# Row sums of squares for the input RMSNorm: from transposed tiles, vector additions and matmuls with ones, to a token-major load with ScalarE's row sums

## The chip, the core and the metric

The kernel runs on one core of a Trainium2 chip. The metric is the device time of one execution in microseconds (us). A core has five engines with a queue each: TensorE (PE in the profile, with its weight loads as PEld), VectorE (DVE), ScalarE (ACT), GpSimd (POOL) and SyncE (SP, which here only issues DMAs). Each engine takes its instructions in the order in which the program holds them; an instruction that waits for a semaphore holds up everything behind it in its queue.

## The reference, cut to what matters

One step of a one-layer encoder with two mixing branches (retention and sliding-window attention), cross attention and SwiGLU, for 1024 prompt tokens and 64 sample tokens, each of 1024 features, in fp32. The change touches only the first norm:

```
def rms_norm(x, g=None):
    y = xf * lax.rsqrt(jnp.mean(xf * xf, axis=-1, keepdims=True) + EPS)
    if g is not None:
        y = y * g
xn = rms_norm(x, g_attn); rq, rk, rv, rg, sq, sk, sv, ga, gb = split(xn @ w_in)
```

So for each of the 1088 tokens one number is wanted, 1 / sqrt(mean of squares + 1e-6). It is a factor per token, and a projection is linear, so the kernel projects x times the gains and multiplies by this factor later.

## The kernel before, in words

The activations lie transposed: features on the 128 partitions, tokens along the row, 8 tiles of 128 x 1088 (T = 1088 tokens; HALF = 544, HC = 272). fp32 products are made of three passes: `split` writes a high part by a ScalarE copy (L123) and a low part by a VectorE subtraction (L124), and TensorE multiplies high by high, high by low and low by high (L222, L223, L225). Each pair of weight blocks of 1024 x 128 goes through seven block products of Strassen's kind (`strassen`; the products are called P1, P2, P6, P5, P7, P3, P4 in the order in which they run). One product is 24 matmuls into a pair of PSUM banks (tile pq), of which three pairs exist. Its operands are the halves of x (tiles B.., T..) and a weight operand `wq` that VectorE's sums (L190, L192, L195, L196) and the split have made from two raw tiles (`raw`, two buffers, filled by SP's DMAs). The results are taken by VectorE (u, L269, and stage, L609); for queries and keys the rotary products follow on VectorE (L640 to L646).

`project_phase` runs: values of head 0, keys of head 0 (w_k), **token_squares**, queries of head 0 (w_q), **token_roots** and `retention_setup`, the retention of head 0 and **spread_roots**, then for each further head its keys, queries, values and SWA queries and its retention, then the gates. What is produced goes by DRAM (d_qkv) to the retention, which loads it in blocks of 256 tokens (ks, qs, vf), transposes keys and values on TensorE (pk) and multiplies them by token factors (`tok`, made of `rtok`) on their way out of PSUM.

The order in which the engines get these instructions isn't that of the code. `build` makes the context with `schedule_with_timeline_sim=True`: a scheduler places every instruction in its engine's queue by its own estimate of times, `rsqrt` under `high_priority`, some pieces tied by `issue_after`. A tile of a pool with `bufs=1` and a tag has one buffer, and a load into it waits until the last reader of the former tile of that tag is done.

The norm's part before the change: `token_squares` loads x a second time from xT in 16 tiles of 128 x 544 (into the buffers of the retention's kt, vb, ss, st), ScalarE squares them (L487), and VectorE adds 14 of them into `rstd` (L489; the first of each half is written there directly), so that rstd holds 128 partial sums for each token. `token_roots` adds over the partitions and turns tokens onto partitions at once, with nine matmuls of rstd against a column of ones (L498, tile pt), and takes the roots (`rsqrt`: L309 VectorE, L310 ScalarE's Sqrt with its table load, L311 to L314 VectorE) into `rtok` (token on the partition, nine columns). `spread_roots` (L508, L510) later spreads rtok back over the partitions into rstd.

Of the kernel before, what the change touches and what calls it, by code (L numbers as in the profile page):

```python
# [11 lines left out]
F32 = mybir.dt.float32  # L12
F32R = mybir.dt.float32r
AF = mybir.ActivationFunctionType
ALU = mybir.AluOpType
# [4 lines left out]
P = 128  # L20
D = 1024
KT = D // P
SEQ = 1024
SMP = 64
# [16 lines left out]
HALF = T // 2  # L41
# [68 lines left out]
class Kernel:  # L110
# [366 lines left out]

    def token_squares(self):

        nc, tags = self.nc, ("kt", "vb", "ss", "st")  # L480
        for t in range(2):
            hs = slice(t * HALF, (t + 1) * HALF)
            for k in range(KT):
                x = self.ra.tile([P, HALF], F32, tag=tags[k % 4], bufs=1, name="xsq")
                self.load(x, self.io["xT"][k, :, hs])
                acc = self.rstd[:, hs]
                nc.scalar.activation(x if k else acc, x, AF.Square)  # L487
                if k:
                    nc.vector.tensor_tensor(out=acc, in0=acc, in1=x, op=ALU.add)  # L489

    def token_roots(self):

        nc = self.nc
        ps = self.norm_psum("pt")
        pv = ps[:, :18].rearrange("p (t two) -> p t two", two=2)
        for i in range(9):
            w = P if i < 8 else SMP
            nc.tensor.matmul(pv[:w, i, :], self.rstd[:, i * P:i * P + w], self.ones[:, :2], start=True, stop=True)  # L498
        self.rsqrt(self.rtok[:, :8], pv[:, :8, 0], D)
        self.rsqrt(self.rtok[:SMP, 8:], pv[:SMP, 8:, 0], D)  # L500

    def spread_roots(self):

# [1342 lines left out]
```

## Time and profile before

| what | value |
|---|---|
| median of three runs | 2179.87 us (2178.16 to 2180.32) |
| the profiled execution, its own time | 2174.66 us |
| its span, first to last instruction | 2172.7 us |
| TensorE busy, of the span | 2140.9 us (99%) |
| TensorE weight loads busy | 2088.6 us (96%) |
| VectorE, ScalarE, GpSimd busy | 72%, 40%, 26% |
| mean granted TensorE clock | 0.995 |

The profiled execution is 5.21 us below the median of the runs, and its span ends 1.96 us below its own time. A busy share is an average: 99% of TensorE says that the program is a stream of matmuls nearly without holes. A matmul is shown with some 0.29 us, but the next one starts 0.125 us after it, since they are pipelined; so time lost on TensorE is read from the starts, not from the durations. The names of rows are those of the program without buffer numbers (pq<-T,wq is a product into pq of operands T and wq).

### The profile page before, as it was taken

The page shows a single profiled execution, that of the slowest core. Times are in us where ns is not written, and L with a number is a line of the kernel's source. Part 1 is how long each engine was busy: PE and PEld are TensorE (multiplying, and loading weights), DVE is VectorE, ACT ScalarE, POOL GpSimd, SP SyncE. Part 2 cuts the span into 40 slices and gives each one's busy share as a digit, 9 for nine tenths or more (in the row PEclk, how much of TensorE's full clock was granted, in tenths as well). Part 3 has the DMA queues.
Part 4 walks back from the last instruction along what each step waited for, and adds up shares of the span by engine and source line. Part 5 has one row for each costly group of instructions (what it writes and reads, how often), then busy time and mean ns, then how long its engine had stood idle before and what let it go on. Part 6 is the DMA issues. An engine that isn't in the chain of part 4 may idle for free.

```text
span 2172.7 us, 41775 instructions
## 1 busy us (share of the span) xinstructions
PE 2140.9 (99%) x16389; PEld 2088.6 (96%) x16389; DVE 1555.6 (72%) x2884; ACT 876.0 (40%) x1898; POOL 559.1 (26%) x438
## 2 busy tenths in 40 slices
PE   9999999999999999999999999999999999999997
PEld 9999999999999997889999999999999999999997
DVE  8996879776677667656545565768777776777588
ACT  7344344344344356653233343333222322344243
POOL 0000311132243223430000000015555555523531
PEclk9999999999999999999999999999999999999999
DMA  6433444445345477327443111422343333394333
GB/s 208 162 130 106 141 133 120 141 131 154 112 145 174 163 220 222 122 77 228 130 155 103 40 57 51 153 81 91 126 133 105 105 98 119 100 328 138 125 109 119
DMA packets 181446, 290.83 MB, mean 134 GB/s; under 512 B 40291, under 2 KB 109315, under 8 KB 181251
## 3 DMA queue, kind: packets, MB, share of 16 engines
q1 hardware_dynamic: 176130, 278.18, 40.5%
q10 hardware_dynamic: 4608, 8.36, 1.0%
q8 instruction: 129, 2.11, 0.4%
q0 software_dynamic: 512, 1.64, 0.2%
q14 instruction: 67, 0.54, 0.1%
HBM read 196.95 MB, written 91.16 MB: 133 GB/s over the span
## 4 chain that ended last, share of the span: by engine, by line
PE 72%; DVE 4%; DMA 2%; issue 2%; ACT 1%; POOL 1%; SPq 0%; POOLq 0%; DVEq 0%; ACTq 0%
PE pq L225 14%; PE pq L222 14%; PE pq L223 14%; PE pd L156 8%; PE pd L158 8%; PE pd L157 8%; PE pss L984 1%; PE pout L1047 1%; DVE wq L124 1%; PE pp L1023 1%; DMA ld<-d_swa 0%; DVE y L1577 0%; PE css L157 0%; PE css L156 0%; PE css L158 0%
## 5 line engine op out<-in xcount | busy, mean ns | idle before, releaser
L124 DVE TENSOR_TENSOR wq<-raw,wq 128x512 fp32r<-128x512 f32 (+1 forms) x499 | 440.1, 887 | 120.5 <-ACT wq L123 116.9
L123 ACT CAST wq<-raw 128x512 fp32r<-128x512 f32 (+1 forms) x499 | 301.7, 613 | 523.9 <-PE pq L225 206.0
L222 PE MATMUL pq<-T,wq 128*128 128x272 f32 x1832 | 490.9, 288 | 2.3 <-ACT wq L123 2.0
L223 PE MATMUL pq<-T,wq 128*128 128x272 f32 x1832 | 491.5, 288 | 0.0
L223 PE MATMUL pq<-B,wq 128*128 128x272 f32 x1592 | 427.5, 289 | 1.9 <-DVE B L124 1.7
L222 PE MATMUL pq<-B,wq 128*128 128x272 f32 x1592 | 426.1, 288 | 0.5 <-ACT B L123 0.4
L225 PE MATMUL pq<-T,wq 128*128 128x272 f32 x1832 | 382.3, 289 | 1.6 <-DVE wq L124 1.6
L222 PEld LDWEIGHTS pq<-T,wq 128*128 128x128 f32 x1832 | 344.2, 188 | 3.6 <-ACT wq L123 2.1
L223 PEld LDWEIGHTS pq<-T,wq 128*128 128x128 f32 x1832 | 344.1, 188 | 0.8 <-issue 0.8
L225 PE MATMUL pq<-B,wq 128*128 128x272 f32 x1592 | 332.9, 289 | 0.0
L223 PEld LDWEIGHTS pq<-B,wq 128*128 128x128 f32 x1592 | 299.7, 188 | 2.9 <-DVE B L124 2.5
L222 PEld LDWEIGHTS pq<-B,wq 128*128 128x128 f32 x1592 | 299.5, 188 | 1.4 <-ACT B L123 0.9
L225 PEld LDWEIGHTS pq<-T,wq 128*128 128x128 f32 x1832 | 289.3, 189 | 3.3 <-DVE wq L124 2.0
L200 POOL TENSOR_TENSOR raw<-raw 128x512 f32<-128x512 f32 (+1 forms) x44 | 63.4, 1442 | 829.1 <-DVE rs_r L311 483.5
L225 PEld LDWEIGHTS pq<-B,wq 128*128 128x128 f32 x1592 | 252.3, 190 | 0.8 <-issue 0.8
L269 DVE TENSOR_TENSOR u<-pq,u 128x544 f32<-128x544 f32 x177 | 127.2, 719 | 90.0 <-PE pq L225 90.0
L615 POOL TENSOR_TENSOR stage<-stage,rstd 128x544 f32<-128x544 f32 x20 | 32.2, 1616 | 341.3 <-ACT rstd L510 216.6
L609 DVE TENSOR_TENSOR stage<-pq,u 128x544 f32<-128x544 f32 x112 | 80.4, 718 | 35.8 <-PE pq L225 27.4
L156 PE MATMUL pd<-xc,wq 128*128 128x256 f32 (+1 forms) x256 | 74.5, 291 | 0.0
L158 PE MATMUL pd<-xc,wq 128*128 128x256 f32 (+1 forms) x256 | 74.1, 289 | 0.0
L1495 POOL TENSOR_TENSOR stage<-stage,rstd_f 128x544 f32<-128x544 f32 x40 | 63.9, 1608 | 39.1 <-ACT stage L1494 39.1
L157 PE MATMUL pd<-xc,wq 128*128 128x256 f32 (+1 forms) x256 | 73.7, 288 | 0.0
(387 smaller groups left out, 4568.2 us busy)
## 6 DMA issues: line engine op xcount, KB each, us to landing
hl<-d_op SPq DMA_DIRECT2D x85, 272.0 KB, 5.2
d_qkv<-stage SPq DMA_DIRECT2D x44, 272.0 KB, 2.1
d_op<-stage SPq DMA_DIRECT2D x44, 272.0 KB, 2.2
d_op<-ht SPq DMA_DIRECT2D x44, 272.0 KB, 3.4
raw<-w_gate SPq DMA_DIRECT2D x22, 512.0 KB, 3.5
raw<-w_up SPq DMA_DIRECT2D x22, 512.0 KB, 4.0
raw<-w_down SPq DMA_DIRECT2D x16, 512.0 KB, 5.1
d_gate<-stage ACTq DMA_DIRECT2D x28, 272.0 KB, 3.0
```

What stands on the lines that cost most here:

```text
L123: self.last_cast = self.nc.scalar.copy(hi, src).ins
L124: return self.nc.vector.tensor_tensor(out=lo, in0=src, in1=hi.bitcast(F32), op=ALU.subtract).ins
L156: mm(ps, wh, xh, start=start, stop=False)
L157: mm(ps, wh, xl, start=False, stop=False)
L158: self.last_mm = mm(ps, wl, xh, start=False, stop=stop).ins
L200: tt(out=a11, in0=a11, in1=a21, op=sub)
L222: mm(ps[:, c, :HC], w[:, 0, ks], x[:, 0, cs], start=start, stop=False)
L223: mm(ps[:, c, :HC], w[:, 0, ks], x[:, 1, cs], start=False, stop=False)
L225: self.last_mm = mm(ps[:, c, :HC], w[:, 1, ks], x[:, 0, c * HC:(c + 1) * HC], start=False, stop=stop).ins
L269: add = lambda out, a, b: nc.vector.tensor_tensor(out=out, in0=a, in1=b, op=ALU.add)
L609: nc.vector.tensor_tensor(out=o, in0=ps, in1=sb, op=ALU.add)
L1495: nc.gpsimd.tensor_tensor(out=g, in0=g, in1=r[t], op=ALU.mult)
```

## The change

x is given to the program a second time with tokens on the rows (`x`, 1088 x 1024, made on the host beside xT). `token_squares` loads it in nine tiles of 128 tokens x 1024 features (the last of 64 tokens), five buffers in turn (kt, vb, st, ks, qs in place of kt, vb, ss, st), and one ScalarE instruction for each squares it and writes the row sums into a column of rtok. `token_roots` takes the roots in place. The 14 additions on VectorE and the nine matmuls with ones are gone, and so is the PSUM tile pt.

```diff
     def token_squares(self):
-        nc, tags = self.nc, ("kt", "vb", "ss", "st")
-        for t in range(2):
-            hs = slice(t * HALF, (t + 1) * HALF)
-            for k in range(KT):
-                x = self.ra.tile([P, HALF], F32, tag=tags[k % 4], bufs=1, name="xsq")
-                self.load(x, self.io["xT"][k, :, hs])
-                acc = self.rstd[:, hs]
-                nc.scalar.activation(x if k else acc, x, AF.Square)
-                if k:
-                    nc.vector.tensor_tensor(out=acc, in0=acc, in1=x, op=ALU.add)
-
-    def token_roots(self):
-        nc = self.nc
-        ps = self.norm_psum("pt")
-        pv = ps[:, :18].rearrange("p (t two) -> p t two", two=2)
+        nc, tags = self.nc, ("kt", "vb", "st", "ks", "qs")
         for i in range(9):
             w = P if i < 8 else SMP
-            nc.tensor.matmul(pv[:w, i, :], self.rstd[:, i * P:i * P + w], self.ones[:, :2], start=True, stop=True)
-        self.rsqrt(self.rtok[:, :8], pv[:, :8, 0], D)
-        self.rsqrt(self.rtok[:SMP, 8:], pv[:SMP, 8:, 0], D)
+            x = self.ra.tile([P, D], F32, tag=tags[i % 5], bufs=1, name="xsq")[:w]
+            self.load(x, self.io["x"][i * P:i * P + w])
+            nc.scalar.activation(x, x, AF.Square, accum_out=self.rtok[:w, i:i + 1])
+
+    def token_roots(self):
+        for r in (self.rtok[:, :8], self.rtok[:SMP, 8:]):
+            self.rsqrt(r, r, D)
...
+    arr["x"] = x
     arr["xT"] = np.ascontiguousarray(x.T).reshape(KT, P, T)
```

The scheduler places the instructions anew from there on. On SP, POOL, DVE and ACT the order differs from token_squares to the end of the third head's retention, and after it only in a swap or two; the matmuls are the same but for the nine. Lines behind token_squares have numbers lower by ten in the changed kernel. Three places matter below.

SP's queue behind the rope table: the loads of x (xsq), the mask and the first values of the retention, and the two raw tiles of the queries' weights (w_q). Before, and then with the change:

```order
L117 DMA rope<-c_rope 128x2x544 x2
L117 DMA xsq<-xT 128x544 x4
L117 DMA dm<-c_dmask 128x448
L117 DMA vf<-d_qkv 128x2x256
L117 DMA xsq<-xT 128x544 x2
L117 DMA raw<-w_q 128x1024 x2
L117 DMA xsq<-xT 128x544 x7
```

```order
L117 DMA rope<-c_rope 128x2x544 x2
L117 DMA xsq<-x 128x1024 x5
L117 DMA dm<-c_dmask 128x448
L117 DMA vf<-d_qkv 128x2x256
L117 DMA xsq<-x 128x1024 x2
L117 DMA raw<-w_q 128x1024 x2
L117 DMA xsq<-x 128x1024
L117 DMA xsq<-x 64x1024
```

Ahead of w_q stand seven loads of 512 KB where six of 272 KB stood, and behind it two where ten stood.

ScalarE's queue from the second group of squares to the roots; raw_825 and raw_790 are the first raw tile of w_q, wq_829 and wq_794 the operand of its first product P1, wq_837 and wq_802 that of P6. Before, and then with the change:

```order
L487 ACTIVATE xsq_770<-xsq_770 128x544
L487 ACTIVATE xsq_774<-xsq_774 128x544
L487 ACTIVATE xsq_778<-xsq_778 128x544
L487 ACTIVATE xsq_782<-xsq_782 128x544
L123 CAST wq_829<-raw_825 128x512
L123 CAST wq_833<-raw_825 128x512
L487 ACTIVATE xsq_786<-xsq_786 128x544
L487 ACTIVATE xsq_790<-xsq_790 128x544
L487 ACTIVATE rstd_68<-xsq_794 128x544
L487 ACTIVATE xsq_809<-xsq_809 128x544
L123 CAST wq_837<-raw_825 128x512
```

```order
L485 ACTIVATE xsq_778,rtok_71<-xsq_778 128x1024
L485 ACTIVATE xsq_781,rtok_71<-xsq_781 128x1024
L123 CAST wq_794<-raw_790 128x512
L123 CAST wq_798<-raw_790 128x512
L485 ACTIVATE xsq_784,rtok_71<-xsq_784 128x1024
L485 ACTIVATE xsq_787,rtok_71<-xsq_787 64x1024
L310 ACT_TABLE_LOAD
L310 ACTIVATE rtok_71<-rs_v_1022 128x8
L123 CAST wq_802<-raw_790 128x512
L123 CAST wq_805<-raw_792 128x512
```

The casts of w_q's P1 and P2 stand behind the seventh square (four more of the same kind stand ahead of the two shown), and the ninth square, the table load and the root have moved ahead of the cast for P6.

VectorE's queue around the same operands; pq_695 and pq_729 are the last two products of w_k. Before, and then with the change:

```order
L489 TENSOR_TENSOR rstd_68<-rstd_68,xsq_778 128x544
L124 TENSOR_TENSOR wq_829<-raw_825,wq_829 128x512
L124 TENSOR_TENSOR wq_833<-raw_825,wq_833 128x512
L641 TENSOR_TENSOR stage1_553<-stage0_552,rope_557 128x544
L190 TENSOR_TENSOR raw_827<-raw_827 128x512
L489 TENSOR_TENSOR rstd_68<-rstd_68,xsq_782 128x544
L609 TENSOR_TENSOR stage0_552<-pq_695,u5_563 128x544
L643 TENSOR_TENSOR stage0_552<-stage0_552,rope_557 128x544
L192 TENSOR_TENSOR raw_825<-raw_827,raw_825 128x512
L489 TENSOR_TENSOR rstd_68<-rstd_68,xsq_786 128x544
L609 TENSOR_TENSOR stage1_553<-pq_729,u3_562 128x544
```

```order
L599 TENSOR_TENSOR stage1_553<-pq_729,u3_562 128x544
L635 TENSOR_TENSOR stage0_552<-stage0_552,stage1_553 128x544
L124 TENSOR_TENSOR wq_794<-raw_790,wq_794 128x512
L124 TENSOR_TENSOR wq_798<-raw_790,wq_798 128x512
L190 TENSOR_TENSOR raw_792<-raw_792 128x512
L631 TENSOR_TENSOR stage1_553<-stage1_553,rope_557 128x544
L309 TENSOR_SCALAR rs_v_1022<-rtok_71 128x8
L192 TENSOR_TENSOR raw_790<-raw_792,raw_790 128x512
L633 TENSOR_TENSOR stage1_553<-stage1_553,rope_557 128x544
L309 TENSOR_SCALAR rs_v_1030<-rtok_71 64x1
L635 TENSOR_TENSOR stage0_552<-stage0_552,stage1_553 128x544
L311 RECIPROCAL rtok_71<-rtok_71 128x8
```

The low part of P1's operand (wq_829, now wq_794) stood ahead of the taking of w_k's last two products; now it stands behind the last of them (pq_729) and one rotary sum. The first steps of the root (L309, L311) have come up between w_q's operands.

## The prediction, made before the changed kernel was run

> **What bounds the kernel now.** I read the page's busy times, then the busy time by stage, then who TensorE waits for, and then the order of time at each place that the change touches.
>
> ```profile
> PE 2140.9 (99%) x16389; PEld 2088.6 (96%) x16389; DVE 1555.6 (72%) x2884; ACT 876.0 (40%) x1898; POOL 559.1 (26%) x438
> 50.00:100.00 50.00, 50.00 (x404) 49.97 (x404) 50.00 (x88) 20.43 (x36) 0.00 (x0) 1.00 0.52 172
> L489 DVE TENSOR_TENSOR rstd<-rstd,xsq 128x544 f32<-128x544 f32 x14 | 10.1, 719 | 0.5 <-ACT xsq L487 0.5
> ...
> 62.18 0.72 DVE L609 TENSOR_TENSOR stage<-pq,u 128x544 f32<-128x544 f32 x1
> 62.82 0.71 DVE L640 TENSOR_TENSOR stage<-stage,rope 128x544 f32<-128x544 f32 x1
> ```
>
> TensorE is the bound of the whole. In the stretch of the changed code, 50 to 100 us, TensorE and VectorE (third busy figure) are both full, ScalarE has 20 of 50 us and GpSimd nothing. VectorE's rows of this shape follow each other after 0.64 us (62.18, 62.82), so the 14 additions hold it for 14 x 0.64 = 9.0 us. A full VectorE costs only where TensorE waits for it, and it does so just behind this stretch:
>
> ```profile
> 111.00 0.41 PE L225 MATMUL pq<-B,wq 128*128 128x272 f32 x2
> 112.14 0.39 PE L222 MATMUL pq<-T,wq 128*128 128x272 f32 x1 [0.72 <-ACT wq L123]
> ...
> 114.52 0.28 PE L223 MATMUL pq<-T,wq 128*128 128x272 f32 x1
> 115.44 0.51 PE L225 MATMUL pq<-T,wq 128*128 128x272 f32 x2 [0.63 <-DVE wq L124]
> ```
>
> The cadence would have put these starts at 111.25 and 114.65 (0.125 us a matmul), so 0.89 and 0.79 us are lost, 1.7 us in all: a queries' operand of the second head is late because VectorE is behind.
>
> **Removed from TensorE: the nine matmuls with ones.**
>
> ```profile
> 67.28 0.95 PE L498 MATMUL pt<-ones,rstd 128*128 128x2 f32 x8
> 68.08 0.50 PE L225 MATMUL pq<-T,wq 128*128 128x272 f32 x2
> 68.42 0.29 PE L222 MATMUL pq<-T,wq 128*128 128x272 f32 x1
> ...
> 89.67 1.16 PE L498 MATMUL pt<-ones,rstd 128*128 128x2 f32 x10
> 90.75 0.52 PE L225 MATMUL pq<-T,wq 128*128 128x272 f32 x2
> 91.11 0.28 PE L222 MATMUL pq<-T,wq 128*128 128x272 f32 x1
> ```
>
> They are 18 passes in two groups. From start to start the groups take 0.80 and 1.08 us, and the pair behind each 0.34 and 0.36 instead of 0.25: 2.1 us of slots. TensorE waits for nothing there, so I take all: **-2.1 us**. It is worth 0 only if VectorE, not TensorE, sets the pace through this stretch; the 9.0 us taken off VectorE in the same stretch speak against that.
>
> **Removed from VectorE: 9.0 us.** It lies beside TensorE's work and counts by what it lets catch up, the 1.7 us above: between -1.7 and 0. In the new order no addition stands ahead of these operands and I count the queue as caught up: **-1.7 us**. The rest of the 9.0 becomes idle time of VectorE.
>
> **Moved on VectorE: w_q's first operand.** TensorE's rows around the border of w_k and w_q, and VectorE's split of P1 and P2 and its last taking of w_k before:
>
> ```profile
> 56.60 1.29 DVE L124 TENSOR_TENSOR wq<-raw,wq 128x512 fp32r<-128x512 f32 x2
> ...
> 60.06 0.41 PE L225 MATMUL pq<-T,wq 128*128 128x272 f32 x2
> 60.31 0.29 PE L222 MATMUL pq<-B,wq 128*128 128x272 f32 x1
> ```
>
> The split was 3.7 us early. Now it stands behind the taking of w_k's last product, which can't start before that product is out: its last pair starts at 60.06 and ends by 60.47, and a signal's time later is 60.6. Then 0.64 (L599), 0.64 (L635) and 0.69 for the split itself give 62.55. TensorE starts w_q at 60.31 with high parts; P1 and P2 are interleaved in fours, so the low part is wanted after eight matmuls, at 61.3. A wait of 62.55 - 61.3 = **+1.25 us**. Behind this split on VectorE stand P2's split and L190, which are wanted later. Its lower end is 0, if the scheduler's pieces slip by each other; the upper end hangs on the loads, next.
>
> **Moved on SP and ScalarE: can w_q be cast in time?**
>
> ```profile
> 47.70 0.66 ACT L487 ACTIVATE rstd<-xsq 128x544 f32<-128x544 f32 x1 [2.05 <-DMA xsq<-xT]
> 55.90 1.14 ACT L123 CAST wq<-raw 128x512 fp32r<-128x512 f32 x2 [1.90 <-DMA raw<-w_q]
> 87.55 1.28 ACT L310 ACT_TABLE_LOAD   x1
> L310 ACT ACTIVATE rtok<-rs_v 128x8 f32<-128x8 f32 x1 | 0.2, 211 | 4.1 <-DVE rs_v L309 4.1
> L870 ACT ACTIVATION_READ_ACCUMULATOR ret_o<-po 128x1 f32 x32 | 6.3, 197 | 0.0
> 41.00:63.00 22.00, 22.00 (x177) 21.98 (x177) 21.42 (x35) 11.17 (x19) 0.00 (x0) 1.00 0.79 268
> 45.00:50.00 5.00, 5.00 (x42) 4.97 (x41) 4.45 (x8) 2.92 (x7) 0.00 (x0) 1.00 1.01 363
> rope<-c_rope SPq DMA_DIRECT2D x2, 544.0 KB, 4.2
> xsq<-xT SPq DMA_DIRECT2D x16, 272.0 KB, 3.5
> d_qkv<-stage SPq DMA_DIRECT2D x11, 272.0 KB, 2.1
> ks<-d_qkv SPq DMA_DIRECT2D x2, 256.0 KB, 3.8
> ```
>
> No row shows a square of 1024 elements. 8 elements take 0.21 us and 544 take 0.66, so 0.84 ns for each, and 1024 take 1.06 us, with 0.2 for the read of the sum 1.26; twice the 544 gives 1.5. Ahead of w_q's first tile SP now sends the rope table (1.11 MB), seven tiles of x (3.67), mask and values (0.49), 5.8 MB with that tile itself. At 363 GB/s, what the fullest five microseconds moved, from 42.5 on (the first issue at 40.5 and 2 us), it lands at 58.5; at 268, the mean of 41 to 63 with idle gaps in it, at 64.1. I take 363 to 350, about 59, because the queue never runs dry: five tiles are sent at once, and the sixth and seventh wait only for the first two squares. Before, the first square began at 47.70 behind 1.39 MB; now 0.25 MB later, 48.3. Then 1.3 for it, three casts of w_k (1.7), and six squares at 1.3 end at 59.1. The casts follow at 59.2 and end by 60.3, when TensorE wants them: +0 us.
>
> P6's operand hangs on a longer chain, since L309 waits for the eighth square ahead of L192, and L311 for ScalarE's root behind the ninth square and the table load: 62 for the eighth tile, 64.6 for two squares, 1.28 + 0.2 to 66.1, then L311, L195, L636 and the split at 0.64 each, 68.4. TensorE wants that low part after 40 more matmuls and eight, at 62.55 + 5 + 1 = 68.5. So +0, without room: each microsecond by which the last loads of x come later than this is one of TensorE.
>
> The keys' store and load again for the first retention block: its last sum on VectorE ends at 67.7, store 2.1, load 3.8 give 73.8 with issue; TensorE reaches the transposes, now inside w_q's products, at 74.0. **+0.2 us**, between 0 and 1.5.
>
> **Everything behind, 120 to 520 us.** The retention of three heads is threaded anew between the products. What TensorE waits for there today:
>
> ```profile
> PE po L156 <- DVE ret_t L884: 1.4, 2, 1.2
> PE po L156 <- ACT ss L123: 0.6, 1, 0.6
> PE po L158 <- DVE ss L124: 0.6, 1, 0.6
> PE pss L156 <- DVE rr L311: 0.3, 1, 0.3
> ...
> 258.64 3.55 POOL L645 TENSOR_TENSOR stage<-stage,stage 128x544 f32<-128x544 f32 x2 [1.33 <-DVE stage L642]
> 259.12 1.85 DVE L124 TENSOR_TENSOR wq<-raw,wq 128x512 fp32r<-128x512 f32 x1
> 260.89 1.88 DVE L643 TENSOR_TENSOR stage<-stage,rope 128x544 f32<-128x544 f32 x1
> ```
>
> 2.9 us in five waits. They sit where VectorE's rows take 1.85 us instead of 0.7 beside GpSimd's rotary sums. The changed kernel has the same GpSimd sums, so I take **0**, from -2.9 (none is met) to +3 (as many again). [...]
>
> **The sum.** -2.1 - 1.7 + 1.25 + 0 + 0.2 + 0 = -2.35 us on the profiled execution of 2174.66 us, 2172.3. The median of the runs shown lies 5.21 higher, so 2179.87 - 2.35 = **2177.5 us**: by 0.11% less, within the 0.2% (4.4 us) that a measurement of this kernel tells from no change.
>
> **Rivals.**
> 1. Faster: the waits of 1.7 and of 2.9 us both go, and VectorE, no longer full, meets w_q too. -2.1 - 1.7 - 2.9 = -6.7 without the new wait, -5.3 with it: about 2173.9. For it: VectorE has 9 us of room just before. Against: the GpSimd sums stay.
> 2. Hidden: VectorE keeps the pace, now by waiting inside its queue for squares and root, and returns what TensorE saved: 0, 2179.9. Against it is the 3.7 us by which w_q's split was early although VectorE was full.
> 3. Slower: the last tiles of x come late. To the ninth 7.1 MB are sent; P6's low part is ready 5.2 us after it, against 67.3 without any wait. At 268 GB/s it lands at 69.0 and TensorE loses 6.9, in place of 1.25: +3.3. From 258 GB/s down the time is over 0.2% more; at 220, 12.7 lost, +9.1, 2189. For it: SP stands still between loads, as these wait for squares and buffers. Against: 363 GB/s is seen with smaller loads.
> 4. The re-threaded retention meets more such waits: +3 on top, 2180.5; only some twelve of today's mean size (2.9 / 5) would pass 0.2%.
>
> **How the numbers follow.** Forecast 0.42 (0.04 of it beyond -0.2%), rival 1 0.32, rival 2 0.08, rival 3 0.13, rival 4 beyond 0.2% 0.05. Faster 0.36, same 0.46, slower 0.18. The likeliest case alone spans 2175.5 to 2179.5; the range reaches to rival 1's -6.7 with 0.7 for the spread of the runs, and up to rival 3 at some 230 GB/s: 2172.5 to 2186.5.
>
> **What would show it.** Right: no row of L498 or L489, VectorE below 90% in 50 to 100 us, a wait of some 1.2 us before w_q's first L225 near 61, no wait near 112, nine squares of 1.06 us with a read of 0.2. Wrong: a wait of TensorE at w_q's P6 near 67 of several us (late loads), a wait at the transposes near 74 over 1.5, or a sum of waits in 120 to 520 far from 2.9.

## The result, and the profile after

| | median | lowest to highest |
|---|---|---|
| before | 2179.87 us | 2175.3 to 2185.74 |
| changed | 2173.66 us | 2168.15 to 2180.3 |

The ratio is 0.9974, 95% interval [0.9966, 0.9982]: faster by 0.26%, some 6 us. A second measurement beside the kernel before gave 0.9964 [0.995, 0.9978]. The time lies in the range that was given, but past the 0.2% of the likeliest case, and the gain is about 2.6 times its 2.35 us. In number it is rival 1.

The two profiled executions don't show this gain: their spans are 2172.7 and 2173.1 us, since the profiled execution of before (2174.66 us) was below every timed run of its kernel. So places are read from the traces, and sizes from the timed runs. Busy times of the changed kernel, then its stretch from 50 to 100 us (columns: length, PE, PEld, DVE, ACT and POOL busy with counts, granted clock, DMA share, GB/s):

```profile
PE 2139.7 (98%) x16371; PEld 2088.6 (96%) x16371; DVE 1546.5 (71%) x2870; ACT 876.2 (40%) x1900; POOL 562.2 (26%) x438
```

```profile
50.00:100.00 50.00, 48.88 (x392) 48.66 (x391) 45.90 (x98) 24.31 (x47) 0.00 (x0) 1.00 0.53 188
```

VectorE has 9.1 us less in the whole program (1555.6 before), TensorE 18 passes less. The squares, by line, and ScalarE's order of time around w_q's first casts:

```profile
L485 ACT ACTIVATE xsq<-xsq 128x1024 f32<-128x1024 f32 (+1 forms) x9 | 9.5, 1054 | 6.7 <-DMA xsq<-x 6.6
L485 ACT ACTIVATION_READ_ACCUMULATOR xsq<-xsq 128x1 f32 (+1 forms) x9 | 1.7, 186 | 0.0
```

```profile
58.67 1.06 ACT L485 ACTIVATE xsq<-xsq 128x1024 f32<-128x1024 f32 x1
59.64 0.19 ACT L485 ACTIVATION_READ_ACCUMULATOR xsq<-xsq 128x1 f32 x1
59.93 1.14 ACT L123 CAST wq<-raw 128x512 fp32r<-128x512 f32 x2
```

The squares last 1.06 us with 0.19 for the read, as worked out, and the casts come at 59.93 us (59.2 had been said). VectorE and TensorE at the border of w_k and w_q:

```profile
61.22 0.72 DVE L599 TENSOR_TENSOR stage<-pq,u 128x544 f32<-128x544 f32 x1
61.85 0.71 DVE L635 TENSOR_TENSOR stage<-stage,stage 128x544 f32<-128x544 f32 x1
62.48 1.29 DVE L124 TENSOR_TENSOR wq<-raw,wq 128x512 fp32r<-128x512 f32 x2
```

```profile
61.81 0.28 PE L223 MATMUL pq<-B,wq 128*128 128x272 f32 x1
63.22 0.51 PE L225 MATMUL pq<-B,wq 128*128 128x272 f32 x2 [1.12 <-DVE wq L124]
```

The low part stands behind w_k's last product, and TensorE loses 63.22 - 61.81 - 0.125 = 1.28 us there. The chain of waits has nothing near 112 and 115 us any more. From 110 to 520 us TensorE waits for two things (the first table), and the first of them, the third head's keys, is followed by matmuls at half the granted clock (the second, by time: 0.50 from 331.4 to 334.4):

```profile
PE pk L738 <- DMA ks<-d_qkv: 2.0, 1, 2.0
PE pss L156 <- DVE rr L311: 1.5, 1, 1.5
```

```profile
325.00:330.00 5.00, 3.11 (x25) 2.89 (x24) 1.96 (x3) 0.64 (x2) 0.00 (x0) 1.00 0.99 270
331.40:334.40 3.00, 3.00 (x15) 3.00 (x14) 3.00 (x7) 2.82 (x9) 0.00 (x0) 0.50 0.33 87
335.00:340.00 5.00, 5.00 (x43) 5.00 (x42) 4.88 (x13) 1.99 (x5) 0.00 (x0) 1.00 0.20 63
```

One more place has changed, and the prediction had no term for it: the sliding-window phase near 810 us, behind everything that was edited. GpSimd's order of time there, before and then changed:

```profile
812.66 0.91 POOL L1006 TENSOR_TENSOR t<-t,den 128x256 f32<-128x256 f32 x1 [2.86 <-DVE den L1004]
813.53 0.58 POOL L1180 DMA_DIRECT2D d_mv<-swin  x1
814.11 0.55 POOL L1181 DMA_DIRECT2D o_mv<-swin  x1
```

```profile
809.24 0.54 POOL L1170 DMA_DIRECT2D d_mv<-swin  x1
809.77 0.55 POOL L1171 DMA_DIRECT2D o_mv<-swin  x1
812.59 0.91 POOL L996 TENSOR_TENSOR t<-t,den 128x256 f32<-128x256 f32 x1 [2.26 <-DVE den L994]
```

The stores of the last values stood behind a softmax product; the scheduler has put them ahead of it. On SP, a load of a gate tile into the buffer that o_mv sends from had to wait for that store; behind the load stood the next queries (d_sq) and the first store of d_mix, which the new order sends earlier, too (d_sq at 820.9 us before and 816.8 us changed, d_mix at 821.3 and 815.0 us). SP's wait in the profile of before, between 800 and 845 us:

```profile
SPq L117 <- DMA o_mv<-swin: 5.3, 1, 5.3
```

The changed kernel has no such wait there.

### The profile page after: what moved, and what is told of

It reads as the page before. It is cut to its first block, busy times and chain, and to the rows that moved or that the text cites. A ratio compares the mean times of both kernels' runs of the same rounds, so it can differ in the third digit from the quotient of the medians.

```text
span 2173.1 us, 41702 instructions
## 1 busy us (share of the span) xinstructions
PE 2139.7 (98%) x16371; PEld 2088.6 (96%) x16371; DVE 1546.5 (71%) x2870; ACT 876.2 (40%) x1900; POOL 562.2 (26%) x438
## 4 chain that ended last, share of the span: by engine, by line
PE 88%; DVE 5%; DMA 3%; ACT 2%; issue 2%; POOL 0%; SPq 0%; POOLq 0%; DVEq 0%; ACTq 0%
PE pq L225 18%; PE pq L223 18%; PE pq L222 18%; PE pd L156 8%; PE pd L158 7%; PE pd L157 7%; PE pout L1037 1%; PE pss L974 1%; DVE wq L124 1%; DMA hl<-d_op 1%; PE pk L738 1%; PE pp L1013 1%; DMA ld<-d_swa 1%; PE po L158 1%; PE po L157 1%
## 5 line engine op out<-in xcount | busy, mean ns | idle before, releaser
L225 PE MATMUL pq<-T,wq 128*128 128x272 f32 x1832 | 384.0, 290 | 0.9 <-DVE wq L124 0.9
L225 PE MATMUL pq<-B,wq 128*128 128x272 f32 x1592 | 332.2, 289 | 1.1 <-DVE wq L124 1.1
L225 PEld LDWEIGHTS pq<-T,wq 128*128 128x128 f32 x1832 | 290.7, 190 | 2.4 <-DVE wq L124 1.1
L225 PEld LDWEIGHTS pq<-B,wq 128*128 128x128 f32 x1592 | 252.4, 190 | 2.5 <-DVE wq L124 1.3
L269 DVE TENSOR_TENSOR u<-pq,u 128x544 f32<-128x544 f32 x177 | 127.2, 719 | 80.9 <-PE pq L225 80.7
```

Of the source, the lines that this page charges most:

```text
L225: self.last_mm = mm(ps[:, c, :HC], w[:, 1, ks], x[:, 0, c * HC:(c + 1) * HC], start=False, stop=stop).ins
L269: add = lambda out, a, b: nc.vector.tensor_tensor(out=out, in0=a, in1=b, op=ALU.add)
```

## The experiments

Theory A is the prediction's: the gain is the work and the waits removed between 40 and 120 us, with what follows from them up to 520 us. Theory B: the waits fall anew in every execution, and the rest is accident. Theory C came out of the first four runs: a good part of the gain is the exchange near 810 us. Each ratio is to the kernel before on the same chip, with its 95% interval.

**The two kernels again.** No edit.

> The kernel before, unchanged, for a second profile and for the granted clock of each of its runs. Removed work (theory A: the gain is the two waits of 1.7 us at w_q's second head, the 2.1 us of slots of the matmuls with ones, and fewer of the 2.9 us of waits behind 120 us): ratio 1.000, and the profile again shows the waits near 112 and 115 us and some 2.9 us of waits between 120 and 520 us. New order (theory B: the gain is accident, waits of TensorE and half-clock stretches behind them fall differently from run to run): ratio 1.000 too, but the second profile's waits between 120 and 520 us differ from the first's 2.9 us by several us, and the number of half-clock stretches varies among runs by one or more.

> The changed kernel, unchanged, beside the kernel before on this chip, for a second profile. Theory A: ratio 0.9972 again, the wait of 1.1 us ahead of w_q's first low part near 61 us is there again, and so are the places of the waits behind 120 us. Theory B: ratio 0.9972 too, but the wait of 2.0 us at 330 us (the load of the third head's keys) is gone or stands elsewhere, since it hangs on when one transfer lands, and the mean granted clock of the runs, rather than the waits, orders their times.

Measured: 0.9999 [0.9989, 1.0008] and 0.9964 [0.995, 0.9978]. The waits stand at the same places again (before: 1.0 and 0.6 us near 112 and 115, the same four between 120 and 520 us with 2.9 us in all; changed: 1.1 us near 61, 3.4 us on the keys, 1.5 us on L311). So they belong to the order, and theory B falls for these places; the sizes vary by up to 1.4 us. Behind 800 us theory B has a point: the two profiles of before differ most there. TensorE waits 2.2 us for a tile swin in the first and 5.5 us in the second, and between 795 and 850 us it has half the clock for 6.8 and for 10.2 us. The second profile of before:

```profile
SPq L117 <- DMA o_mv<-swin: 4.7, 1, 4.7
```

```profile
838.68 0.69 PE L156 MATMUL pd<-ret,wq 128*128 128x384 f32 x1 [5.52 <-ACT swin L963]
```

**VectorE's additions put back, without matmuls with ones.**

```diff
             nc.scalar.activation(x, x, AF.Square, accum_out=self.rtok[:w, i:i + 1])
+            for t in range(2 if i < 7 else 0):
+                acc = self.rstd[:, t * HALF:(t + 1) * HALF]
+                nc.vector.tensor_tensor(out=acc, in0=acc if i else x[:, :HALF], in1=x[:, D - HALF:], op=ALU.add)
```

> The changed kernel with 14 additions of 128x544 on VectorE put back between the squares (into a tile whose sum is not used), nothing else: VectorE's 9.0 us of the stretch from 50 to 100 us come back, no matmul with ones does. Theory A: TensorE waits for w_q's operands again, the 1.7 us near 112 us or their like, and the wait near 61 us stays or grows: 2 to 5 us over the changed kernel, ratio to the kernel before 0.998 to 0.9995. Theory B: the additions lie beside TensorE's work as any filler would, within 1 us of the changed kernel, ratio 0.997.

Measured: 0.998 [0.9971, 0.9989], 1 to 3.5 us over the changed kernel, though the intervals overlap. Its waits from 40 to 520 us and its stretch from 50 to 100 us:

```profile
PE pq L225 <- DVE wq L124: 3.3, 2, 3.2
PE pq L222 <- ACT wq L123: 1.1, 1, 1.1
PE pb L875 <- ACT ret_o L869: 0.6, 1, 0.6
PE pq L222 <- DVE u L269: 0.4, 1, 0.4
```

```profile
50.00:100.00 50.00, 45.18 (x339) 44.35 (x338) 49.65 (x105) 23.30 (x45) 0.00 (x0) 0.93 0.46 159
```

VectorE is full, TensorE waits for its operands and then runs at half clock for a while (0.93 in the mean). In the trace the additions are no filler. But what they cost there, some 7 us by 125 us (below), is mostly given back: the order that follows has neither the wait on the keys nor that on L311.

**The additions alone taken from the kernel before.** Seven eighths of the squares are left out of the sums, so the roots are of the wrong size.

```diff
                 nc.scalar.activation(x if k else acc, x, AF.Square)
-                if k:
-                    nc.vector.tensor_tensor(out=acc, in0=acc, in1=x, op=ALU.add)
```

> The kernel before without its 14 additions on VectorE (the sums then hold the first eighth of the squares alone), all else as before: loads, squares, matmuls with ones, order of w_k and w_q. Theory A: the waits near 112 and 115 us go, none comes near 61 us: 1.7 to 3 us under the kernel before, ratio 0.9986 to 0.9992, and the 2.1 us of the matmuls with ones stay. Theory B: ratio 0.9990 to 1.001, with waits behind 120 us at other places than in the kernel before.

Measured: 0.9958 [0.9945, 0.997], some 9 us, the whole gain of the change or more with the matmuls still in. TensorE's waits from 40 to 520 us in it:

```profile
PE pb L880 <- ACT ret_o L874: 1.9, 2, 1.2
PE pq L222 <- DVE u L269: 0.2, 1, 0.2
```

They are 2.1 to 2.4 us less than in the two profiles of the kernel before; that explains a quarter of the 9. This kernel, the changed one and the one with additions put back, all faster than before, share one thing behind 520 us: the new order of stores near 810 us. This is theory C. (With the additions put back SP still stands 4.0 us on o_mv, in two waits: the new order doesn't always take this wait away.)

**The exchange alone, in the kernel before.**

```diff
-                nc.gpsimd.tensor_tensor(out=p, in0=p, op=ALU.mult,
-                                        in1=den.rearrange("p v i -> p (v i)").unsqueeze(2).broadcast_to([P, 4, n]))
+                by = den.rearrange("p v i -> p (v i)").unsqueeze(2).broadcast_to([P, 4, n])
+                mul = lambda: nc.gpsimd.tensor_tensor(out=p, in0=p, op=ALU.mult, in1=by)
+                if (c, hf) == (0, 1):
+                    self.late_mul = mul
+                else:
+                    mul()
...
-                nc.gpsimd.dma_start(io["o_mv"][t * P:(t + 1) * P, h * 256:(h + 1) * 256], o)
+                kept = nc.gpsimd.dma_start(io["o_mv"][t * P:(t + 1) * P, h * 256:(h + 1) * 256], o).ins
+                if t:
+                    with tc.issue_after(kept):
+                        self.late_mul()
```

> The kernel before with one pair of rows exchanged on GpSimd in the phase behind the retention: the two stores of the last values (L1180, L1181, second half) are issued ahead of the softmax product of 128x256 (L1006) that they stood behind; every other engine's order is that of the kernel before. In two profiles of the kernel before, SP's load of a gate tile stands 5.3 and 4.7 us for the store of L1181 there, and TensorE then waits 2.2 and 5.5 us near 835 us; in the changed kernel, whose scheduler put the stores first, neither is seen. Theory C (about half of the gain or more came from this exchange, 750 us behind the edited lines): 2.5 to 5 us under the kernel before, ratio 0.9977 to 0.9989, SP's wait gone, TensorE's wait at that place under 1.5 us. Theory A (the gain is the work removed at 40 to 120 us and its waits): ratio 1.000 within 0.0005.

Measured: 0.9983 [0.9973, 0.9993], 1.5 to 5.9 us faster, with no line of the norm touched. GpSimd's order of time:

```profile
809.01 0.54 POOL L1184 DMA_DIRECT2D d_mv<-swin  x1
809.54 0.55 POOL L1185 DMA_DIRECT2D o_mv<-swin  x1
812.34 0.91 POOL L1007 TENSOR_TENSOR t<-t,den 128x256 f32<-128x256 f32 x1 [2.25 <-DVE den L1004]
```

SP's wait on o_mv is gone. TensorE's wait near 835 us is not under the 1.5 us that had been expected: 2.16 us, beside 2.23 and 5.52 in the two profiles of before. The last 12500 matmuls stand in the same order in all kernels, so their starts can be compared one by one. From the 10255th to the 9789th from the end (some 780 to 850 us) TensorE takes 71.0 us with the exchange, beside 70.0 and 74.1 in the two profiles of before; the changed kernel takes 69.4 and 69.5. That is about 1 us less in the mean, less than the two profiles of one kernel differ. So where on TensorE the 3.7 us come back isn't shown by any profile; the timed runs carry them, and their granted clocks give a hint: the mean of the listed clocks is 0.9964 (12 runs) against 0.9952 (32 runs of before), by which an estimate gives 0.0012 x 2175 = 2.6 us less lost at half clock.

**The exchange put back in the changed kernel**, first the stores alone (`self.mul` is GpSimd's last softmax product):

```diff
-                nc.gpsimd.dma_start(self.d_mv[h, :, t, :], o)
-                nc.gpsimd.dma_start(io["o_mv"][t * P:(t + 1) * P, h * 256:(h + 1) * 256], o)
+                with tc.issue_after(self.mul if t else self.values_out):
+                    nc.gpsimd.dma_start(self.d_mv[h, :, t, :], o)
+                    nc.gpsimd.dma_start(io["o_mv"][t * P:(t + 1) * P, h * 256:(h + 1) * 256], o)
```

> The changed kernel with that one pair of rows put back as in the kernel before: the stores behind the softmax product; on SP one load of a gate tile moves by one place with it, all else is the changed kernel. Theory C: 2.5 to 5 us over the changed kernel, ratio to the kernel before 0.9985 to 0.9995, and SP's load stands some 5 us for the store again. Theory A: the changed kernel's own ratio, 0.9964 to 0.9974.

Then SP's part with it, and the same whole in the kernel without additions. The held store sends what a later load has put into its tile, so one tile of d_mix isn't the product in these two.

```diff
-                        self.load_queries(qTs, 4)
+                        with tc.issue_after(self.load_queries(qTs, 4)):
+                            self.held_mix()
...
-                self.store(self.d_mix[m, :, c0:c0 + n], g[:, :n])
+                put = lambda m=m, c0=c0, n=n, g=g: self.store(self.d_mix[m, :, c0:c0 + n], g[:, :n])
+                if step == 2:
+                    self.held_mix = put
+                else:
+                    put()
```

> The changed kernel with the whole late place put back as it was in the kernel before, not the stores on GpSimd alone: behind them, SP sends the second gate tile, the queries and only then the first product's store (held back by hand), as before; one gate load stays a place early. All up to 800 us is the changed kernel. With the stores alone put back, the ratio was 0.9979, no more than half of what the exchange in the kernel before was worth (0.9983). Theory C, whole (what counts is the store for which SP's queue stands together with what is queued behind it): 2.5 to 5 us over the changed kernel, ratio 0.9985 to 0.9997. Theory C, half (the late place explains only 1 to 2 us of the 6): ratio 0.997 to 0.9982.

> The kernel before without its 14 additions (the roots are taken of the mean over the first 128 of the 1024 channels, so that values keep their size), with the late place held as in the kernel before by the same means. Without that hold it gave 0.9958. Theory C: what is left is the early part alone, 2.6 us in the profiles up to 500 us: ratio 0.998 to 0.9993. Theory A: 0.9955 to 0.997, as without the hold.

Measured: 0.9979 [0.9967, 0.999]; whole 0.9984 [0.9976, 0.9993]; without additions 0.9972 [0.9962, 0.9982] (0.9958 with the new order). SP stands 4.6, 4.4 and 4.8 us on o_mv in their profiles. Against the changed kernel's 0.9974 and 0.9964 the whole costs 2 to 4 us and the stores alone 1 to 3; against its own counterpart the third costs 3 us. The first lies between what theories A and C had asked for, the whole between C's two cases. Each of these intervals touches its counterpart's, so none of the three shows it by itself; all go the way, and whole near the size, of the exchange in the kernel before. What the whole leaves, 0.9984, is the worth of all that changed ahead of 800 us in timed runs: 3.5 us (1.5 to 5.2). The third leaves 0.9972, 6.1 us (3.9 to 8.3), where theory C had asked for 0.998 to 0.9993: taking the additions out is worth some 3.5 us more than the 2.6 us that the profile up to 500 us gave. Where these come from isn't shown.

**The matmuls put back, with the new place of the stores held** (by the edit shown above).

```diff
     def token_roots(self):
-        for r in (self.rtok[:, :8], self.rtok[:SMP, 8:]):
-            self.rsqrt(r, r, D)
+        ps = self.norm_psum("pt")
+        pv = ps[:, :18].rearrange("p (t two) -> p t two", two=2)
+        for i in range(9):
+            w, j = P if i < 8 else SMP, min(i, 7)
+            nc.tensor.matmul(pv[:w, i, :], self.ident[:, :w], self.rtok[:, j:j + 2], start=True, stop=True)
+        self.rsqrt(self.rtok[:, :8], pv[:, :8, 0], D)
+        self.rsqrt(self.rtok[:SMP, 8:], pv[:SMP, 8:, 1], D)
```

> The changed kernel with nine small matmuls put back between the squares and the roots (identity by the column of sums, into PSUM, from where the roots are taken, so that they cost TensorE what the matmuls with ones did), and with the stores' place of the changed kernel held by hand, since the scheduler would otherwise turn it back. Theory A and C alike price these matmuls at the 2.1 us of slots of the prediction; the new order puts w_q's first split earlier, so that the wait of 1.1 us near 61 us may go: +0.8 to +2.1 us over the changed kernel, ratio 0.997 to 0.9985. If they lie in time that TensorE has anyway: 0, ratio 0.9964 to 0.997.

Measured: 0.9972 [0.9962, 0.9981], within 2 us of the changed kernel. The wait near 61 us and that on the keys are both gone. So in the time the 2.1 us of slots can't be told from what the other order saves. The profile tells them apart: counted as in the next section, the 941st matmul starts 0.85 us later than in the changed kernel, about the nine matmuls' 2.1 us less the 1.3 us of the wait near 61 us.

**Three and four buffers for x, the stores' place held.**

```diff
-        nc, tags = self.nc, ("kt", "vb", "st", "ks", "qs")
+        nc, tags = self.nc, ("kt", "vb", "st")
...
-            x = self.ra.tile([P, D], F32, tag=tags[i % 5], bufs=1, name="xsq")[:w]
+            x = self.ra.tile([P, D], F32, tag=tags[i % 3], bufs=1, name="xsq")[:w]
```

(With four, "ks" stays in the list.)

> The changed kernel with three buffers for the tiles of x instead of five, so that the squares run one behind the other's load and w_q's split is not put behind w_k's last product on VectorE, and with the stores' place of the changed kernel held by hand. Theory A: the wait of 1.3 us near 61 us goes and the retention is threaded in another order, without the third head's late keys at 330 us (2.0 and 3.4 us and a half-clock stretch of 1.7): 1.3 to 5 us under the changed kernel, ratio to the kernel before 0.994 to 0.9965. If the late tiles of x take the place of that wait (rival 3 of the prediction): TensorE waits near 67 us and the time is over the changed kernel's.

> The changed kernel with four buffers for the tiles of x, the stores' place held as in the changed kernel. As three buffers (0.9989), it should take the wait of 1.3 us near 61 us away; three gave it back by 0.5 to 1.3 us at each of four of the retention's products and by the late keys at 330 us. If that was the three buffers' order: 1 to 3 us under the changed kernel, ratio 0.995 to 0.9965. If a new order of the retention meets waits of this size whatever it is: 0.997 to 0.999.

Measured: 0.9989 [0.998, 0.9998] and 1.0004 [0.9995, 1.0013], both slower than the changed kernel, though both lose less than 0.3 us at w_q's first operands. Part of what takes it back is the wait on the keys at 330 us, here in the profile with three and then with four, the last with the half clock behind it:

```profile
PE pk L738 <- DMA ks<-d_qkv: 3.2, 1, 3.2
```

```profile
PE pk L738 <- DMA ks<-d_qkv: 5.1, 1, 5.1
```

```profile
332.00:337.00 5.00, 5.00 (x24) 5.00 (x24) 4.15 (x9) 3.63 (x10) 0.00 (x0) 0.50 0.21 87
```

The last square ends at 66 us, so the buffers can act on 330 us only by the order that follows. Another part lies behind 800 us: between 800 and 860 us TensorE waits 5.1 us for ScalarE's tiles swin in both profiles (3.4 and 1.7 us, 3.5 and 1.6), beside 1.2 to 2.0 us in those of the changed kernel, although the stores keep their new place. So this place alone doesn't fix what the phase costs; why these waits are longer here isn't shown.

**That one load moved.**

```diff
-            self.load(kraw, src(1, c0, BLK))
+            if (h, b) == (2, 1):
+                with self.tc.issue_after(self.scaled):
+                    nc.gpsimd.dma_start(kraw, src(1, c0, BLK))
+            else:
+                self.load(kraw, src(1, c0, BLK))
```

(`self.scaled` is GpSimd's last product in `project`.)

> The changed kernel with one load moved: the keys of the third head's second block, for which TensorE waited 2.0 and 3.4 us near 330 us in two profiles, and which stood on SP behind the queries' stores of 64 and 32 columns, go out on GpSimd's queue behind its last product. TensorE's order up to that place is the changed kernel's. If that wait, with the half-clock stretch behind it (1.7 us), is what the new order gave back of the early gain: 3.5 to 5 us under the changed kernel, ratio to the kernel before 0.994 to 0.9955, no wait on those keys and no half-clock stretch near 331 us. If the next thing is late instead (values, queries, or a product's result): within 1.5 us of the changed kernel, 0.9965 to 0.9975.

Measured: 0.997 [0.9958, 0.9981], no better than the changed kernel by its time, though its profile is 1.8 us ahead of the changed kernel's at 500 us (counted as in the next section). The wait on the keys and the half clock behind it are gone, and the next things are late, 0.7 us on L865 and 1.2 more on L311:

```profile
PE pss L156 <- DVE rr L311: 2.7, 2, 1.5
PE pk L738 <- ACT ret_o L865: 0.7, 1, 0.7
```

No version here beats the changed kernel by more than the intervals allow.

## Why the prediction was right, and where it was wrong

TensorE's matmuls, too, stand in another order from some 52 us to the end of the retention, which the text on the change doesn't say. To put traces of different orders side by side: I count TensorE's matmuls back from the end of the retention, where all orders are alike again, each at the median distance of its shape in the profile of before. The first three rows give the time at which the same work is left; the last is the start of the first common matmul (the 12500th from the end), read directly.

| | before (3 profiles) | changed (2) | adds put back | before without adds |
|---|---|---|---|---|
| near 125 us | 125.3, 125.6, 124.5 | 123.4, 122.9 | 130.1 | 124.5 |
| near 330 us | 330.7, 330.9, 329.6 | 326.6, 326.1 | 332.7 | 327.6 |
| near 345 us | 345.7, 346.0, 344.8 | 345.4, 346.3 | 347.9 | 342.7 |
| first common matmul | 500.3, 500.6, 499.5 | 499.0, 499.6 | 501.2 | 497.6 |

(The third profile of before is the one with the exchange, which is the same up to here.)

- Matmuls with ones, -2.1, and the two waits, -1.7, less +1.25 and +0.2: -2.35. The waits are gone, the new wait is 1.28 us (a signal's time, put at 60.6 - 60.47 = 0.13 us in the forecast of it, is 0.03 to 0.05 us in two rows of the changed kernel: L269 starts at 146.41 and 99.44 us, behind L225 pairs that end at 146.38 and 99.39), and the lead at 125 us is 125.1 - 123.1 = 2.0 us. The start of an execution varies (the 261st matmul starts at 40.22 us before and at 40.84 us in the changed kernel); without it, from the 261st matmul (some 41 us) to the 941st, those with ones left out, TensorE takes 88.6, 88.8 and 87.4 us before and 85.9 in both profiles of the changed kernel: 2.3 us less. The 20 matmuls around each group of ones take 3.38 and 3.68 us before, 2.52 and 2.48 changed, so the groups cost 0.86 + 1.20 = 2.1 us. Right as a sum, and near in its large terms.
- w_q's casts and P6 at +0: right. The casts came 0.7 us later than said and in time; no wait near 67 us. Rival 3 fell.
- Keys' store and load at 74: no wait there. Right.
- VectorE below 90% between 50 and 100 us: it is at 92%. The 9.1 us went, but other work moved up.
- Waits from 120 to 520 us, 0 (-2.9 to +3): the old ones are all gone, as rival 1 had it, and the lead grows to 4 us at 330. Then the wait on the keys and the half clock take it back. In the profiles about 1 us of it is left at 500 us. The 0 was near by luck, by two large terms against each other, of which the prediction named neither. Its reason, that the GpSimd sums stay, is an argument that no run shows: VectorE's rows beside them are as slow in the changed kernel (1.89 us below, 1.85 and 1.88 before), yet none of the five waits is left there. The new one of 1.5 us, at 236 us, does stand behind a row that is slow beside such a sum: L309 takes 1.30 us from 233.91, and the rows of the same 128x2 behind it 0.15 to 0.16.

```profile
262.96 1.82 POOL L635 TENSOR_TENSOR stage<-stage,stage 128x544 f32<-128x544 f32 x1 [1.13 <-DVE rr L318]
```

```profile
263.47 1.89 DVE L633 TENSOR_TENSOR stage<-stage,rope 128x544 f32<-128x544 f32 x1
```

- **The step that failed is the end of the sum at 520 us.** The text on the change says that the order differs behind the retention "only in a swap or two"; those got no price. One of them is the exchange near 810 us. Made alone it gives 3.7 us (1.5 to 5.9) in timed runs; put back whole it takes 2 to 4.

In timed runs the part ahead of 800 us is worth 3.5 us (1.5 to 5.2, with the late place put back whole), which holds the 2.35 of the forecast, and the exchange 3.7; together they fit the 6.2 us within their intervals. The profiles show less of both: about 1 us at 500 us, and about 1 us near 810. Which waits the timed runs have isn't known, as they leave no trace of them; so how the rest reaches TensorE stays open. The forecast of 2177.5 was thus short by a term that none of its cases had, and rival 1's number (2173.9 against 2173.66) was met by accident: its waits went, but were replaced.

## What to carry to other kernels

Where a scheduler places instructions by estimated times, compare the whole order, to the end of the program, and price each exchange in a queue for which something waits, however far it is from the edited lines. When work is taken off a full engine, its value is what comes late without it, and the next thing that is late takes part of it back. A profile of one execution gives places; gains of a few parts in a thousand need many timed runs and the exchange made alone.

## What was not expected of the hardware

A short wait of TensorE cost more than its length here. In the clock records, each of five waits on the keys of 2.0 to 3.4 us (changed, again, stores put back, whole put back, three buffers) is followed by 3.41 us at half clock, and that of 5.1 us by 6.83; the 1.5 us on L311 is followed by none. By the clock, 3.41 us at half lose 1.7 us; by the starts in the changed kernel (twelve matmuls in 2.72 us from 331.76 us on, 0.227 us each in place of 0.125) it is an estimated 1.5. The length of the wait doesn't decide alone: near 835 us, waits of 1.8 and 1.9 us (stores put back, whole put back) are followed by such a stretch, and waits of 2.2 and 2.3 us (before, matmuls put back) are not. What decides isn't shown. In the changed kernel's profile the three stretches start whole multiples of their length apart (27.38, 331.16 and 809.03 us: 89 and 140 times 3.413).
